# Two heads at once in PEER's routing, one-hots in two operations, and moved gather steps

## The chip, the cores and the metric

One core of a Trainium2 chip runs the kernel. The metric is the device time of one execution in microseconds; the time before is the median of three runs.

## The reference

One decoder layer for 512 tokens of width 1024, in float32: RMSNorm, one combined projection, windowed attention and a gated linear recurrence, their gated merge with a residual, then a PEER layer with its residual and a final RMSNorm. The change touches PEER, which picks 16 of 16384 single-neuron experts per token and head:

```python
def peer_layer(h, w_q, keys, u, v):
    q = (h @ w_q).reshape(B, S, PEER_HEADS, 2, PEER_KEY_DIM)          # 8 heads, two halves
    sc = jnp.einsum('bshpd,phnd->bshpn', q, keys)                     # 128 keys per half
    v1, i1 = lax.top_k(sc[..., 0, :], 16)
    v2, i2 = lax.top_k(sc[..., 1, :], 16)
    cand = v1[..., :, None] + v2[..., None, :]                        # 256 pairs
    best, pos = lax.top_k(cand, 16)
    idx = take_along_axis(i1 * 128 + i2, pos)
    gates = jax.nn.softmax(best)
    act = gelu(einsum('tkd,td->tk', u[idx], h))
    return einsum('tk,tkd->td', gates * act, v[idx])
```

## The kernel before, in words

The layer's first part (projections, attention, recurrence, merge) fills the first 390 us and is not touched, but for the queue of one small load.

PEER is done in two ways. For 160 of the 512 tokens, a block of 128 (`sp0`) and 32 more (`sp1`), the expert rows are gathered: 320 gather steps, each an indirect DMA on POOL of 128 rows of `u` or `v` (L707, 512 KB, four buffers `ga`) and later one step on VectorE that uses them (L715 for `u`, L725 for `v`). `pace` (L727 on) writes gathers up to a given number into the program and, three gathers behind (`GLAG`), their VectorE steps.

For the other 352 tokens (`DT`) the layer is computed densely. For each of 128 chunks of 128 experts, `act_chunk` loads the chunk of `u` (SyncE), splits it into a high part (ScalarE, L142) and a low part (VectorE, L162) and runs 24 matmuls of 352 columns (L646); GELU writes the tile `gel`. The choices of routing become a dense matrix G of gates, 128 by 128 for each token. Then the main loop takes each chunk's `gel` times its slice of G (`w`, L980), splits that too (`whi`, `wlo`), and multiplies it with the chunk of `v` (L994 to L996, 18 matmuls of 512 columns) into six PSUM banks.

The stages in order:

1. Routing (390 to 607 us). For each of 8 heads and 2 halves PE makes queries and scores (L847), VectorE the top 16 of 128 for four token blocks (L854 to L858). After both halves of a head, `route` finds the best 16 pairs: sums of candidates, top 16 of them, softmax on ScalarE, the ranks' arithmetic (L800 to L810), and small float16 one-hots over 16 ranks that pick the key numbers (L816 to L824). It is a generator, resumed by `next(routing)` once per half, so a head's choices run beside the next head's scores. Meanwhile U chunks are written in (`fill`).
2. The G stage (613 to 784). In 22 steps of 16 tokens VectorE writes one-hots of both key numbers over 128 keys (`oh`, L904 to L907, eight tokens at a time; the second is multiplied by the gate's high and low part), PE multiplies them for four tokens at a time into a bank (L912: a weight load and a matmul of 128 columns, 704 of each), ScalarE writes the bank into `G_` (L914), and each step's 1 MB goes to memory (`Gd`, L916). After each bank a quarter of a U chunk's matmuls follows (`piece`). Every third step one gather is added, seven in all.
3. Held U chunks (784 to 819). Of the 53 that there is room for, five (`HELD`) are kept back to cover the last write of Gd and the first read of it (`g_load`, L936). The last two (`LASTU`) are loaded behind that read. Ahead of them `pace(EARLY)` brings the gathers to 16.
4. The main loop, with the remaining U chunks spread over its first 116 chunks and the gathers over all but the last `TAILC`, two.
5. The end: the last three gather steps, then RMSNorm and output of all rows (`final_rows`).

Each engine runs its instructions in the order in which the program has them; the scheduler may interleave what is written, and keeps the matmuls of the G stage in written order. A step that waits on VectorE holds all that is behind it.

Of the kernel before, what the change touches and what calls it, by code (L numbers as in the profile page):

```python
# [6 lines left out]
F32 = mybir.dt.float32  # L7
# [33 lines left out]
QT = 4  # L41
OT = 8
# [7 lines left out]
TAILC = 2  # L50
# [8 lines left out]
def host(inp):  # L59
# [10 lines left out]
    def tm(m):  # L70
# [18 lines left out]
         np.broadcast_to(np.repeat(np.arange(TK, dtype=np.float32), NB), (P, TK * NB)),  # L89
# [27 lines left out]
def layer(nc, tc, a, out, probe=None, upto=99):  # L117
# [37 lines left out]
    def wsplit(raw, shape, parts=1, eng=None):  # L155
        hi = oc.tile(list(shape), F32R, tag="hi", bufs=HB, name=nm("hi"))
        lo = oc.tile(list(shape), F32R, tag="lo", bufs=HB, name=nm("lo"))
        n = shape[1] // parts
        for i in range(parts):
            m = slice(i * n, (i + 1) * n)  # L160
            hi_of(hi[:, m], raw[:, m])
            (eng or V).tensor_tensor(lo[:, m], raw[:, m], hi[:, m].bitcast(F32), op=OP.subtract)  # L162
        return hi, lo
# [28 lines left out]
    with tc.tile_pool(name="front", bufs=1) as fr, tc.tile_pool(name="psf", bufs=1, space=PSUM) as psf:  # L192
# [82 lines left out]
        POOL.dma_start(gm, a["gmix"])  # L275
# [345 lines left out]
    with tc.tile_pool(name="peer", bufs=1) as pp, tc.tile_pool(name="psp", bufs=1, space=PSUM) as psp, ExitStack() as ps:  # L621
# [47 lines left out]

        work = []  # L670

        def piece(limit):
            while len(work) < 2 and nu[0] < limit:
                work.append(act_pieces(next(todo), True))
                next(work[-1])
                nu[0] += 1
            if work and next(work[0], 0) == 0:
                work.pop(0)
# [59 lines left out]
        with tc.tile_pool(name="win", bufs=1) as wp:  # L738
            iota = wp.tile([P, TK, NB], F16, name="iota")
            io32 = wp.tile([P, TK, NB], F32, name="io32")  # L740
            SP.dma_start(io32, a["const"][:, 6 * P:6 * P + TK * NB].rearrange("p (a n) -> p a n", n=NB))
            V.tensor_copy(iota, io32)
            iok32 = wp.tile([P, P, QT], F32, name="iok32")
            SP.dma_start(iok32, a["const"][:, 6 * P + TK * NB:6 * P + TK * NB + P * QT].rearrange("p (i t) -> p i t", t=QT))
# [5 lines left out]
            NK = (P, NB, TK)  # L750

            def route(h, tv, ti):
                hs = slice(h * TK, (h + 1) * TK)
                v1, v2 = tv[:, 0], tv[:, 1]
                cand = w16((P, NB, 64), F32, "cand")
                V.tensor_tensor(cand[:, :, 0:16], v1[:, :, 0:1].to_broadcast([P, NB, 16]), v2, op=OP.add)
                V.tensor_tensor(cand[:, :, 16:40].rearrange("p h (a b) -> p h a b", a=3),
                                v1[:, :, 1:4].unsqueeze(3).to_broadcast([P, NB, 3, 8]),
                                v2[:, :, 0:8].unsqueeze(2).to_broadcast([P, NB, 3, 8]), op=OP.add)
                V.tensor_tensor(cand[:, :, 40:56].rearrange("p h (a b) -> p h a b", a=4),  # L760
                                v1[:, :, 4:8].unsqueeze(3).to_broadcast([P, NB, 4, 4]),
                                v2[:, :, 0:4].unsqueeze(2).to_broadcast([P, NB, 4, 4]), op=OP.add)
                V.tensor_tensor(cand[:, :, 56:64], v1[:, :, 8:16],
                                v2[:, :, 0:1].to_broadcast([P, NB, 8]), op=OP.add)
                best = w16(NK, F32, "best")
                pos = w16(NK, U32, "pos")
                for n in range(NB):
# [18 lines left out]
                k16 = w16((P, 2, TK, NB), F16, "k16")
                for w in range(2):
# [23 lines left out]
                r16 = w16((P, 2, TK, NB), F16, "r16")  # L811
                ACT.activation(r16[:, 0].rearrange("p k n -> p n k"), af, AF.Copy)
                V.tensor_tensor(r16[:, 1].rearrange("p k n -> p n k"), pf, st, op=OP.subtract)
                shape = [P, 2 * TK, TK, NB]
# [6 lines left out]
                                .to_broadcast([P, 2, TK, TK * NB]), op=OP.mult)  # L821
                for m_ in (8, 4, 2):
                    V.tensor_tensor(eq[:, :, 0:m_, :], eq[:, :, 0:m_, :], eq[:, :, m_:2 * m_, :], op=OP.add)
                V.tensor_tensor(i12[:, :, :, hs].rearrange("p w n k -> p w k n"),  # L824
                                eq[:, :, 0, :].rearrange("p (w k) n -> p w k n", w=2),
                                eq[:, :, 1, :].rearrange("p (w k) n -> p w k n", w=2), op=OP.add)
# [3 lines left out]
            for hp in range(2 * PH):  # L830
                h, p_ = divmod(hp, 2)
                if p_ == 0:
                    tv = w16((P, 2, NB, TK), F32, "tv", 3)
                    ti = w16((P, 2, NB, TK), U32, "ti", 3)
# [15 lines left out]
                for n in range(NB):  # L850
                    sc = sb[:, n, :]
                    v_, i_ = tv[:, p_, n, :], ti[:, p_, n, :]
# [6 lines left out]
                if p_ == 1:  # L859
                    routing = route(h, tv, ti)  # L860
# [15 lines left out]
        with tc.tile_pool(name="gb", bufs=1, reuse_waits="tile") as gp:  # L876
# [4 lines left out]
            for n in range(1, NB):  # L881
# [3 lines left out]
                for w in range(2):  # L885
                    PE.transpose(b[:, w, :], i12[:, w, n, :], ident)
# [3 lines left out]
                V.tensor_copy(g16[:, 0, t], gs[:, t])  # L890
                V.tensor_tensor(g16[:, 1, t], gs[:, t], g16[:, 0, t], op=OP.subtract)
            NQ = OT // QT
            shape = [P, NQ, P, QT]
            for s_ in range(NPT):
                G_ = gp.tile([P, NE, TG], F32, tag="G", bufs=2, name=nm("G"))
                for o in range(TG // OT):
                    t = slice(s_ * TG + o * OT, s_ * TG + (o + 1) * OT)

                    def row(x):
                        return x.rearrange("p (q t) -> p q t", t=QT).unsqueeze(2).to_broadcast(shape)  # L900

                    ioq = iok.unsqueeze(1).to_broadcast(shape)
                    oh = gp.tile([P, 3, NQ, P, QT], F16, tag="oh", bufs=2, name=nm("oh"))
                    V.tensor_tensor(oh[:, 0], ioq, row(iT[:, 0, t]), op=OP.is_equal)  # L904
# [142 lines left out]
```

## Time and profile before

| | |
|---|---|
| median of 3 runs | 1666.84 us (1663.52 to 1667.65) |
| the profiled execution, whole | 1675.46 us |
| its span | 1673.7 us |
| PE matmul busy | 1605.2 us, 96% |
| VectorE (DVE) busy | 1321.9 us, 79% |
| ScalarE (ACT) busy | 709.6 us, 42% |
| GpSimd (POOL) busy | 487.3 us, 29% |
| moved by DMA | 400.87 MB, 240 GB/s over the span |

PE is the matmul engine, PEld its weight load. A matmul's row is longer than its share of PE's time, since matmuls overlap; the distance of starts is what one costs. A wait stands in brackets behind the instruction that it delayed, with what ended it. PEclk is the granted share of PE's full clock of 2.4 GHz; 0.50 is 1.2 GHz.

### The profile page before, as it was taken

The page shows a single profiled execution, that of the slowest core. Times are in us where ns is not written, and L with a number is a line of the kernel's source. Part 1 is how long each engine was busy: PE and PEld are TensorE (multiplying, and loading weights), DVE is VectorE, ACT ScalarE, POOL GpSimd, SP SyncE. Part 2 cuts the span into 40 slices and gives each one's busy share as a digit, 9 for nine tenths or more (in the row PEclk, how much of TensorE's full clock was granted, in tenths as well). Part 3 has the DMA queues.
Part 4 walks back from the last instruction along what each step waited for, and adds up shares of the span by engine and source line. Part 5 has one row for each costly group of instructions (what it writes and reads, how often), then busy time and mean ns, then how long its engine had stood idle before and what let it go on. Part 6 is the DMA issues. An engine that isn't in the chain of part 4 may idle for free.

```text
span 1673.7 us, 23435 instructions
## 1 busy us (share of the span) xinstructions
PE 1605.2 (96%) x8511; PEld 1358.7 (81%) x8511; DVE 1321.9 (79%) x2560; ACT 709.6 (42%) x1152; POOL 487.3 (29%) x341
## 2 busy tenths in 40 slices
PE   8999999999999969997899999999999999999996
PEld 6877678888988869997788888887888888888874
DVE  8456663647999988887688888878888888888887
ACT  5433353234554547775333333333333333333333
POOL 4000000000000010002455555445455555554542
PEclk9999999999999979999899999999999999999998
DMA  5311133334333347888999999999999999999984
GB/s 173 101 51 51 51 104 111 103 115 154 108 109 116 103 126 192 219 224 265 336 340 353 349 368 349 337 341 339 344 368 351 359 354 347 360 358 363 343 305 145
DMA packets 197491, 400.87 MB, mean 240 GB/s; under 512 B 103344, under 2 KB 105904, under 8 KB 197376
## 3 DMA queue, kind: packets, MB, share of 16 engines
q1 hardware_dynamic: 58832, 206.02, 35.2%
q0 software_dynamic: 46336, 168.39, 27.0%
q10 hardware_dynamic: 92208, 24.98, 6.1%
q8 instruction: 66, 1.08, 0.3%
q14 instruction: 49, 0.40, 0.1%
HBM read 371.91 MB, written 27.39 MB: 239 GB/s over the span
## 4 chain that ended last, share of the span: by engine, by line
PE 53%; issue 16%; POOL 12%; DVE 12%; DMA 6%; ACT 1%; POOLq 0%; DVEq 0%; SPq 0%; ACTq 0%
PE b L646 13%; POOL ga L707 11%; PE b L263 5%; PE b L262 5%; PE b L995 5%; PE b L996 5%; PE b L265 4%; PE b L994 4%; DMA ga<-v,idx 4%; PE b L912 4%; DVE lo L162 3%; DMA ga<-un,idx 1%; DVE ti L858 1%; DVE mr L856 1%; DVE e L725 1%
## 5 line engine op out<-in xcount | busy, mean ns | idle before, releaser
L707 POOL DMA_INDIRECT ga<-un,idx x160 | 225.2, 1407 | 944.5 <-ACT gs L889 581.3
L646 PE MATMUL b<-hT,hi 128*128 128x352 f32 x2048 | 366.9, 327 | 2.2 <-ACT hi L142 1.7
L646 PEld LDWEIGHTS b<-hT,hi 128*128 128x128 f32 x2048 | 334.4, 190 | 12.7 <-ACT hi L142 2.0
L995 PE MATMUL b<-lo,whi 128*128 128x512 f32 (+1 forms) x768 | 305.0, 397 | 15.0 <-DVE lo L162 14.6
L996 PE MATMUL b<-hi,wlo 128*128 128x512 f32 (+1 forms) x768 | 304.3, 396 | 0.0
L994 PE MATMUL b<-hi,whi 128*128 128x512 f32 (+1 forms) x768 | 302.7, 395 | 0.0
L707 POOL DMA_INDIRECT ga<-v,idx x160 | 240.4, 1502 | 208.3 <-DVE e L725 190.3
L142 ACT ACTIVATE hi<-s 128x1024 fp32r<-128x1024 f32 (+1 forms) x195 | 205.1, 1052 | 203.1 <-PE b L646 88.1
L162 DVE TENSOR_TENSOR lo<-s,hi 128x1024 fp32r<-128x1024 f32 (+1 forms) x195 | 238.5, 1224 | 29.7 <-ACT hi L142 28.0
L142 ACT ACTIVATE whi<-w 128x352 fp32r<-128x352 f32 x128 | 63.7, 498 | 400.0 <-PE b L995 361.2
L725 DVE SCALAR_TENSOR_TENSOR e<-ga,wt,e 128x1024 f32<-128x1024 f32 x158 | 202.2, 1280 | 19.3 <-DMA ga<-v,idx 18.4
L715 DVE SCALAR_TENSOR_TENSOR ga<-ga,h 128x1024 f32<-128x1024 f32 x160 | 194.5, 1220 | 28.6 <-DMA ga<-un,idx 26.9
L646 PE MATMUL b<-hT,lo 128*128 128x352 f32 x1024 | 191.3, 325 | 11.8 <-DVE lo L162 11.8
L995 PEld LDWEIGHTS b<-lo,whi 128*128 128x128 f32 (+1 forms) x768 | 138.8, 181 | 59.2 <-DVE lo L162 22.0
L646 PEld LDWEIGHTS b<-hT,lo 128*128 128x128 f32 x1024 | 168.0, 189 | 12.4 <-DVE lo L162 12.3
L996 PEld LDWEIGHTS b<-hi,wlo 128*128 128x128 f32 (+1 forms) x768 | 138.5, 180 | 39.3
L994 PEld LDWEIGHTS b<-hi,whi 128*128 128x128 f32 (+1 forms) x768 | 138.2, 180 | 35.3 <-ACT hi L142 1.2
L142 ACT ACTIVATE hi<-vr 128x1024 fp32r<-128x1024 f32 x128 | 134.6, 1051 | 75.9 <-PE b L646 46.3
L162 DVE TENSOR_TENSOR lo<-vr,hi 128x1024 fp32r<-128x1024 f32 x128 | 156.1, 1220 | 9.4 <-ACT hi L142 9.4
L263 PE MATMUL b<-hT,hi 128*128 128x512 f32 (+1 forms) x376 | 146.4, 391 | 0.3 <-DVE hT L145 0.3
L262 PE MATMUL b<-hT,hi 128*128 128x512 f32 (+1 forms) x376 | 146.1, 390 | 0.2
L985 DVE TENSOR_TENSOR wlo<-w,whi 128x352 fp32r<-128x352 f32 x128 | 67.0, 523 | 80.9 <-ACT whi L142 77.5
(284 smaller groups left out, 1960.5 us busy)
## 6 DMA issues: line engine op xcount, KB each, us to landing
s<-uc SPq DMA_DIRECT2D x128, 512.0 KB
vr<-vc SPq DMA_DIRECT2D x128, 512.0 KB
Gd<-G ACTq DMA_DIRECT2D x22, 1024.0 KB
gt<-Gd SPq DMA_DIRECT2D x32, 704.0 KB
s<-wfm SPq DMA_DIRECT2D x30, 512.0 KB
s<-wq SPq DMA_DIRECT2D x16, 512.0 KB
s<-wmg SPq DMA_DIRECT2D x8, 512.0 KB
s<-wout SPq DMA_DIRECT2D x8, 512.0 KB
```

Source lines behind the costliest of these rows:

```text
L142: ACT.activation(dst, src, AF.Copy)
L162: (eng or V).tensor_tensor(lo[:, m], raw[:, m], hi[:, m].bitcast(F32), op=OP.subtract)
L262: PE.matmul(b, wh[:, k, :], rh(i), start=start and i == 0, stop=False)
L263: PE.matmul(b, wh[:, k, :], rl(i), start=False, stop=False)
L646: m = PE.matmul(o, w[:, k, :], z[:, k, t], start=i == 0, stop=i == 3 * KD - 1)
L707: tc.keep_in_program_order(POOL.indirect_dma_start(out=t, out_offset=None, in_=a[src], in_offset=bass.IndirectOffsetOnAxis(ap=b.idx[:, j:j ...
L715: V.scalar_tensor_tensor(t, t, 1.0, h20, op0=OP.mult, op1=OP.mult, accum_out=b.act[:, j:j + 1])
L725: V.scalar_tensor_tensor(b.ax, t, b.wt[:, j:j + 1], b.ax, op0=OP.mult, op1=OP.add)
L985: last = V.tensor_tensor(wlo, w, whi.bitcast(F32), op=OP.subtract)
L994: PE.matmul(acc[tb][hf][0:m, :], whi[:, t], vh[:, d], start=i == 0, stop=False)
L995: PE.matmul(acc[tb][hf][0:m, :], whi[:, t], vl[:, d], start=False, stop=False)
L996: PE.matmul(acc[tb][hf][0:m, :], wlo[:, t], vh[:, d], start=False, stop=i == NE - 1)
```

## The change

`route` takes two heads at a time for heads 0 to 5; heads 6 and 7 go singly. Its tiles then hold eight token blocks instead of four, and the top 16 of the candidates, still one block at a time, is cut in two by a second `yield`:

```diff
-            def route(h, tv, ti):
+            def route(h0, tv, ti):
+                NB2 = tv.shape[2]
+                NK = (P, NB2, TK)
+                iota = iotas[NB2]
...
+                    if n == NB - 1 and NB2 > NB:
+                        yield
...
+                two = h < PH - 2
+                if p_ == 0 and not (two and h % 2):
+                    tv = w16((P, 2, NB * (1 + two), TK), F32, "tv", 3)
...
-                if p_ == 1:
-                    routing = route(h, tv, ti)
+                if p_ == 1 and not (two and h % 2 == 0):
+                    for _ in routing:
+                        pass
+                    routing = route(h - two, tv, ti)
```

The one-hots of eight tokens are one tile `[P, 3, P, 8]`, written by two operations. Neighbouring columns of a token's one-hot are now 8 elements of float16 apart, before 4:

```diff
-QT = 4
-OT = 8
+QT = 8
+BT = 4
...
-                    oh = gp.tile([P, 3, NQ, P, QT], F16, tag="oh", bufs=2, name=nm("oh"))
-                    V.tensor_tensor(oh[:, 0], ioq, row(iT[:, 0, t]), op=OP.is_equal)
-                    V.tensor_tensor(oh[:, 2], ioq, row(iT[:, 1, t]), op=OP.is_equal)
-                    V.tensor_tensor(oh[:, 1], oh[:, 2], row(g16[:, 0, t]), op=OP.mult)
-                    last = V.tensor_tensor(oh[:, 2], oh[:, 2], row(g16[:, 1, t]), op=OP.mult)
+                    oh = gp.tile([P, 3, P, QT], F16, tag="oh", bufs=2, name=nm("oh"))
+                    V.tensor_tensor(oh[:, 1:3], ioq, iT[:, :, t].unsqueeze(2).to_broadcast(shape), op=OP.is_equal)
+                    last = V.tensor_tensor(oh[:, 0:2], oh[:, 1:2].to_broadcast(shape),
+                                           g16[:, :, t].unsqueeze(2).to_broadcast(shape), op=OP.mult)
...
-                                lastg = tc.keep_in_program_order(PE.matmul(b[:, i, :], oh[:, 0, q, :, i], oh[:, 1 + w, q, :, i], start=w == 0, stop=w == 1))
+                                lastg = tc.keep_in_program_order(PE.matmul(
+                                    b[:, i, :], oh[:, 2, :, q * BT + i], oh[:, 1 - w, :, q * BT + i],
+                                    start=w == 0, stop=w == 1))
```

Gather steps: one every second step of the G stage (eleven), then one behind each of three held chunks. `piece` may load and split a held chunk ahead of its matmuls:

```diff
-                        piece(KEEP - HELD)
+                        piece(KEEP - HELD, KEEP - HELD + 2)
...
-                pace((s_ + 1) // 3, last.ins)
+                pace((s_ + 1) // 2, last.ins)
...
+        held = cur["lo"]
+        for c_, g_ in work:
+            for _ in g_:
+                pass
+            pace(nga[0] + 1, held.ins)
         with tc.issue_after(lastg.ins):
-            fill(KEEP - nu[0] - LASTU)
+            for _ in range(KEEP - nu[0] - LASTU):
+                fill(1)
+                held = cur["lo"]
+                pace(nga[0] + 1, held.ins)
...
-        pace(EARLY, last.ins)
+        pace(EARLY, held.ins)
```

The end: gathers end three chunks earlier, the gathered block is finished before the last two chunks, and those two are taken bank by bank:

```diff
-TAILC = 2
+TAILC = 5
...
-                    for i, whi, wlo, vh, vl in ready:
-                        for hf in range(2):
-                            d = slice(hf * 512, (hf + 1) * 512)
+                    for hf in range(2):
+                        d = slice(hf * 512, (hf + 1) * 512)
+                        for i, whi, wlo, vh, vl in ready:
...
-        while nsp[0] < NS:
-            sparse(nsp[0])
-            nsp[0] += 1
-        final_rows(ys[0], [sp0.ax[:, 0:512], sp0.ax[:, 512:]], 0, P)
+            if c == NE - 3:
+                while nsp[0] < NS:
+                    sparse(nsp[0])
+                    nsp[0] += 1
+                final_rows(ys[0], [sp0.ax[:, 0:512], sp0.ax[:, 512:]], 0, P)
```

Besides, the constants `io32` and `iok32` are twice as wide, and the load of `gm` at the start is issued by ScalarE instead of POOL.

How the instructions move. VectorE, the last half's maxima of routing (`b_5303` and `b_5173` are its scores) beside head 6's small one-hots (`eq`). Before:

```order
L813 TENSOR_TENSOR r_963_5386<-pf_5238,st_5380 128x4x16
L816 TENSOR_TENSOR eq_5389<-iota,r_963_5386 128x2048
L162 TENSOR_TENSOR lo_5344<-s_955_5341,hi_5343 128x1024
L820 TENSOR_TENSOR eq_5389<-eq_5389,k_935_5235 128x2048
L854 MAX tv_5116<-b_5303 128x8
L823 TENSOR_TENSOR eq_5389<-eq_5389 128x32x32
```

With the change, where the first maximum of `b_5173` stands 24 rows above the first `eq`; this is the block's fourth:

```order
L817 SCALAR_TENSOR_TENSOR st_5250<-af_5244,st_5250 128x64
L870 MAX_INDEX ti_4987<-tv_4986,mr_5278 128x8
L820 TENSOR_TENSOR r_912_5256<-pf_5108,st_5250 128x4x16
L866 MAX tv_4986<-b_5173 128x8
L823 TENSOR_TENSOR eq_5259<-iota_3091,r_912_5256 128x2048
L867 MAX_INDEX ti_4987<-tv_4986,b_5173 128x8
L827 TENSOR_TENSOR eq_5259<-eq_5259,k_884_5105 128x2048
```

Head 6's one-hots and the rank arithmetic moved from before the last half's first maximum to among its maxima.

VectorE, from the last low part of the G stage to the first product with G. `lo` is a U chunk's low part, L715 and L717 are gather steps. Before:

```order
L162 TENSOR_TENSOR lo_7349<-s_1252_7346,hi_7348 128x1024
L715 SCALAR_TENSOR_TENSOR ga_7609,act_3079<-ga_7609,h_62 128x1024
L715 SCALAR_TENSOR_TENSOR ga_7612,act_3079<-ga_7612,h_62 128x1024
L715 SCALAR_TENSOR_TENSOR ga_7615,act_3079<-ga_7615,h_62 128x1024
L715 SCALAR_TENSOR_TENSOR ga_7618,act_3079<-ga_7618,h_62 128x1024
L715 SCALAR_TENSOR_TENSOR ga_7621,act_3079<-ga_7621,h_62 128x1024
L715 SCALAR_TENSOR_TENSOR ga_7624,act_3079<-ga_7624,h_62 128x1024
L162 TENSOR_TENSOR lo_7510<-s_1275_7507,hi_7509 128x1024
L162 TENSOR_TENSOR lo_7542<-s_1279_7539,hi_7541 128x1024
L162 TENSOR_TENSOR lo_7574<-s_1283_7571,hi_7573 128x1024
L980 SCALAR_TENSOR_TENSOR w_7708<-gel_3136,gt_7607 128x352
```

With the change:

```order
L162 TENSOR_TENSOR lo_7149<-s_1205_7146,hi_7148 128x1024
L162 TENSOR_TENSOR lo_7229<-s_1216_7226,hi_7228 128x1024
L717 SCALAR_TENSOR_TENSOR ga_6966,act_3079<-ga_6966,h_62 128x1024
L162 TENSOR_TENSOR lo_7339<-s_1233_7336,hi_7338 128x1024
L717 SCALAR_TENSOR_TENSOR ga_7129,act_3079<-ga_7129,h_62 128x1024
L162 TENSOR_TENSOR lo_7374<-s_1238_7371,hi_7373 128x1024
L717 SCALAR_TENSOR_TENSOR ga_7292,act_3079<-ga_7292,h_62 128x1024
L717 SCALAR_TENSOR_TENSOR ga_7333,act_3079<-ga_7333,h_62 128x1024
L717 SCALAR_TENSOR_TENSOR ga_7368,act_3079<-ga_7368,h_62 128x1024
L1000 SCALAR_TENSOR_TENSOR w_7490<-gel_3138,gt_7410 128x352
```

Three low parts moved up, each ahead of the gather steps that it stood behind, and fewer gather steps are left in the stretch.

VectorE near the end. `lo<-vr` is the low part of a chunk of `v`; L725 and L727 are gather steps, L960 and L980 (with `e` in its name) the additions of `final_rows`. Before:

```order
L985 TENSOR_TENSOR wlo_14974<-w_14970,whi_14972 128x352
L725 SCALAR_TENSOR_TENSOR e_528_3077<-ga_14953,wt_3080,e_528_3077 128x1024
L162 TENSOR_TENSOR lo_14967<-vr_14923,hi_14966 128x1024
L960 TENSOR_TENSOR e_2724_14751<-e_2724_14751,e_528_3077 128x512 x2
L960 TENSOR_TENSOR e_2724_14751<-e_2724_14751,b_7499 128x512
```

With the change, from the last gather step on (`lo_14681` is chunk 124's, and three more follow below):

```order
L727 SCALAR_TENSOR_TENSOR e_528_3077<-ga_14645,wt_3080,e_528_3077 128x1024
L980 TENSOR_TENSOR s_2680_14551<-s_2680_14551,b_14626 32x512
L980 TENSOR_TENSOR s_2680_14551<-s_2680_14551,b_14628 32x512
L162 TENSOR_TENSOR lo_14681<-vr_14596,hi_14680 128x1024
L983 TENSOR_TENSOR rs_14636<-s__2698_14630 32x1
L1005 TENSOR_TENSOR wlo_14688<-w_14684,whi_14686 128x352
L980 TENSOR_TENSOR e_2678_14548<-e_2678_14548,e_528_3077 128x512
```

The last gather step moved from ahead of the last chunk's low part to ahead of that of the fourth from the end, with the gathered rows' final sums behind it.

## Rows read from the trace of the kernel before

**Rows 1.** Windows by stage: start:end length, busy us (instructions) per engine, PEclk, DMA share, GB/s.
```profile
390.00:596.00 206.00, 201.06 (x1118) 182.64 (x1117) 194.26 (x960) 109.06 (x236) 0.00 (x0) 1.00 0.35 115
596.00:613.00 17.00, 2.75 (x13) 2.30 (x14) 13.31 (x35) 7.47 (x27) 3.51 (x3) 0.60 0.30 95
613.00:784.00 171.00, 169.72 (x1229) 157.13 (x1228) 144.89 (x207) 119.15 (x129) 12.25 (x8) 0.99 0.78 213
784.00:819.00 35.00, 22.53 (x124) 21.67 (x122) 19.92 (x30) 10.70 (x15) 14.41 (x10) 0.85 0.96 329
819.00:1640.00 821.00, 810.05 (x4039) 686.65 (x4039) 697.16 (x893) 297.07 (x408) 427.72 (x304) 1.00 0.95 348
1640.00:1674.00 34.00, 19.07 (x71) 13.66 (x69) 22.23 (x34) 10.73 (x29) 9.70 (x1) 0.81 0.34 115
```

**Rows 2.** Timeline of PE after routing: start us, us, engine line op [idle before <-releaser].
```profile
607.29 0.69 PE L886 MATMUL b<-ident,i 128*128 128x128 f32 x2 [11.42 <-DVE i L824]
```

**Rows 3.** Timeline from 784 to 819, and SyncE's waits (total, times, longest).
```profile
799.72 2.71 PE L646 MATMUL b<-hT,lo 128*128 128x352 f32 x8 [10.75 <-DVE lo L162]
...
808.26 0.96 DVE L980 SCALAR_TENSOR_TENSOR w<-gel,gt 128x352 f32<-128x352 f32 x2 [4.51 <-DMA gt<-Gd]
...
818.82 0.40 PE L994 MATMUL b<-hi,whi 128*128 128x512 f32 x1
...
SPq L936 <- DMA Gd<-G: 20.4, 1, 20.4
```

**Rows 4.** Timeline of the last 35 us.
```profile
1639.79 9.91 POOL L707 DMA_INDIRECT ga<-v,idx  x1 [1.89 <-DVE e L725]
...
1653.36 1.28 DVE L725 SCALAR_TENSOR_TENSOR e<-ga,wt,e 128x1024 f32<-128x1024 f32 x1 [4.48 <-DMA ga<-v,idx]
...
1655.84 0.80 PE L995 MATMUL b<-lo,whi 128*128 128x512 f32 x1 [4.04 <-DVE lo L162]
...
1662.71 0.40 PE L996 MATMUL b<-hi,wlo 128*96 128x512 f32 x1
...
1667.34 2.74 DVE L967 SCALAR_TENSOR_TENSOR e<-e,rs,h 128x512 f32<-128x512 f32 x4
```

**Rows 5.** VectorE's groups by shape, 390 to 612 us: count, busy us, mean ns, idle before.
```profile
L816 DVE TENSOR_TENSOR eq<-iota,r 128x2048 f16<-128x2048 f16 x8 | 9.8, 1224 | 0.7
...
L809 DVE TENSOR_TENSOR st<-st,tf 128x64 f32<-128x64 f32 x8 | 1.8, 225 | 0.3
```

**Rows 6.** Timeline of routing's last heads: scores on PE, first maxima and indices on VectorE.
```profile
554.74 1.16 PE L847 MATMUL b<-ky,qp 128*128 128x128 f32 x8 [1.00 <-ACT qp L844]
...
557.93 0.29 DVE L854 MAX8 tv<-b 128x8 f32<-128x128 f32 x1
...
580.30 1.16 PE L847 MATMUL b<-ky,qp 128*128 128x128 f32 x8 [0.84 <-ACT qp L844]
...
583.49 0.29 DVE L854 MAX8 tv<-b 128x8 f32<-128x128 f32 x1
...
607.26 0.49 DVE L865 SCALAR_TENSOR_TENSOR e<-i 128x128 f32<-128x128 f32 x2
```

**Rows 7.** VectorE's first one-hot group by shape, 613 to 784 us; the other three are alike.
```profile
L904 DVE TENSOR_TENSOR oh<-iok,iT 128x1024 f16<-128x1024 f16 x42 | 29.0, 692 | 22.2 <-PE b L912 22.2
```

**Rows 8.** Timeline of weight loads of the one-hots: half clock, then full clock.
```profile
612.70 0.70 PEld L912 LDWEIGHTS <-oh 128*128 128x128 f16 x6 [1.09 <-issue]
...
734.98 0.82 PEld L912 LDWEIGHTS <-oh 128*128 128x128 f16 x8
```

**Rows 9.** ScalarE's groups by shape, 390 to 790 us.
```profile
L914 ACT ACTIVATE G<-b 128x512 f32<-128x512 f32 x88 | 96.0, 1091 | 54.3 <-PE b L912 50.7 <-issue 3.7
...
L844 ACT ACTIVATE qp<-b 128x512 f32<-128x512 f32 x15 | 9.0, 600 | 4.0 <-PE b L265 4.0
```

**Rows 10.** Chain that ended last, pieces: start us, us, what.
```profile
1081.57 3.80 PE b L646 x24
...
1541.08 9.17 DMA ga<-v,idx
```

More of the change, by code (lines that the diff above doesn't have):

```diff
@@ L88, in host @@
          np.full((P, P), 1.0 / P, np.float32),
-         np.broadcast_to(np.repeat(np.arange(TK, dtype=np.float32), NB), (P, TK * NB)),
+         np.broadcast_to(np.repeat(np.arange(TK, dtype=np.float32), 2 * NB), (P, TK * 2 * NB)),
          np.broadcast_to(np.repeat(np.arange(P, dtype=np.float32), QT), (P, P * QT)),
@@ L274, in layer @@
         ktm, logf = [], []
-        POOL.dma_start(gm, a["gmix"])
+        ACT.dma_start(gm, a["gmix"])
         POOL.dma_start(ones, a["const"][:, 5 * P:6 * P])
@@ L670, in layer, with piece @@
         work = []
[L672 to L675, printed above, removed]
+        def piece(limit, ahead):
+            while len(work) < 2 and nu[0] < ahead:
+                c = next(todo)
+                work.append((c, act_pieces(c, True)))
+                next(work[-1][1])
                 nu[0] += 1
-            if work and next(work[0], 0) == 0:
+            if work and work[0][0] < limit and next(work[0][1], 0) == 0:
                 work.pop(0)
@@ L738, in layer @@
         with tc.tile_pool(name="win", bufs=1) as wp:
[L739 to L742, printed above, removed]
+            io32 = wp.tile([P, TK, 2 * NB], F32, name="io32")
+            SP.dma_start(io32, a["const"][:, 6 * P:6 * P + TK * 2 * NB].rearrange("p (a n) -> p a n", n=2 * NB))
+            iotas = {}
+            for n in (NB, 2 * NB):
+                iotas[n] = wp.tile([P, TK, n], F16, name=f"iota{n}")
+                V.tensor_copy(iotas[n], io32[:, :, 0:n])
             iok32 = wp.tile([P, P, QT], F32, name="iok32")
-            SP.dma_start(iok32, a["const"][:, 6 * P + TK * NB:6 * P + TK * NB + P * QT].rearrange("p (i t) -> p i t", t=QT))
+            SP.dma_start(iok32, a["const"][:, 6 * P + TK * 2 * NB:6 * P + TK * 2 * NB + P * QT].rearrange("p (i t) -> p i t", t=QT))
             V.tensor_copy(iok, iok32)
@@ L851, in layer @@
                     sc = sb[:, n, :]
-                    v_, i_ = tv[:, p_, n, :], ti[:, p_, n, :]
+                    n_ = n + NB * (two and h % 2)
+                    v_, i_ = tv[:, p_, n_, :], ti[:, p_, n_, :]
                     m = wp.tile([P, NE], F32, tag="mr", bufs=4, name=nm("mr"))
```

82 lines of the change are left out of this document (39 added, 43 removed).

## The prediction, before the changed kernel ran

> **What bounds the kernel now.** I read the windows by stage first [rows 1]. Look at PE's busy time against each stage's length. From 819 to 1640 us PE is busy 810.05 of 821 us while the DMA engines are busy 0.95 of the time at 348 GB/s. So half of the run is bound by PE, with the transfers close behind it; nothing in the change removes matmuls there. What can be won is PE's idle time elsewhere: 14.2 us from 596 to 613 (2.75 of 17 busy), 12.5 from 784 to 819 (22.53 of 35) and 14.9 from 1640 on (19.07 of 34). The granted clock is 0.60, 0.85 and 0.81 in these three, so after each pause PE also runs for a while at 1.2 GHz. The G stage, 613 to 784, is full: 169.72 of 171 us.
>
> Then I read each hole in the timeline. The first ends when VectorE has written the last expert indices: PE's transposes had waited 11.42 us for it [rows 2]. The second is a wait of 10.75 us of a held U chunk for its low part [rows 3]: VectorE stood in gather steps ahead of that low part in its order. But a second chain runs beside it: SyncE waited 20.4 us for the last write of Gd, and the first product with G, `w`, began only at 808.26 after it [rows 3]. The third is 4.04 us behind the last gather, plus a tail of VectorE work after the last matmul [rows 4].
>
> The profiled execution took 1675.46 us, the median of the three timed runs is 1666.84, so I take 8.6 us off sums made against the profile. About 0.3%, 5 us, is what a measurement of this kernel can tell from no change.
>
> **Part 1: routing for two heads.** For each of three pairs 20 VectorE instructions go away (four for the candidates, the negated best, the reciprocal, eight of the rank arithmetic, six of the small one-hots); their elements stay. An instruction on 64 float32 elements takes 225 ns [rows 5], of which 64 at 0.96 a ns are 67, so 158 ns are saved by each merged one: 60 times 0.158 is 9.5 us of VectorE time. Does it shorten the path? In the last heads both engines turn in the same period: the score matmuls start 25.56 us apart (554.74 and 580.30) and so do the first maxima (557.93 and 583.49), about 2 us after the scores' end [rows 6]. So VectorE can be ahead of PE by 2 us at most before it waits for scores, and PE itself has only 206 minus 201.06, that is 4.9 us, of slack in this stage [rows 1]. Against that, the order shows head 6's small one-hots moved from ahead of the last block's first maximum to behind it. That puts two operations of 1.22 us [rows 5] and six of 0.225, about 3.8 us, into the stretch between the last scores and the indices at 607.26 [rows 6]. Gain and loss cancel; I take 0, with ends of -9.5 (all of the saving lands) and +3.8 (only the move does). If PE does run ahead, it only idles earlier.
>
> **Part 2: one-hots by two operations.** Eight tokens took four operations of 692 ns [rows 7]; two on 2048 elements should take 1.22 each, as the ones of the same size and type do [rows 5]. That is 0.3 us less for 44 groups, 13 us of VectorE time, all beside PE, which is the full engine here; VectorE already waited 22.2 us for PE in this stage [rows 7]. Its cover is PE's 1.9 us per four tokens (171 us over 88 blocks). At the stage's start the first product comes after two long operations instead of three short ones and some casts: -0.6 us.
>
> The price that the trace does not show is on PE. A column of a one-hot now lies 16 bytes from the next, not 8. No PE read with such a step exists in the trace. Below: eight pairs of weight load and matmul take 0.82 us, 102 ns each, although 128 columns at 2.4 GHz are 53 ns; the stream is not what sets the pair, and a slower one may hide: 0. Above: at the half clock, where every column takes twice as long, six loads take 0.70 us, 117 ns each [rows 8]. If both reads halve their rate and overlap as they do there, 704 pairs cost 704 times 0.014, 10 us. ScalarE's rows say that a step can halve a rate: writing G with 64 bytes between elements takes 1091 ns for 512 elements, writing 512 in a row 600 [rows 9]. I take 0, because the nearest row is the pair itself, with half its time unused by the columns.
>
> [...]
>
> **Part 3: gather steps behind held chunks.** Eleven gathers are now issued inside the G stage instead of seven, so five instead of nine are left before the main loop, and on VectorE each held chunk's low part stands before the next gather step. VectorE has room: 144.89 of 171 us busy, minus 13, plus four steps of about 1.2. The wait of 10.75 us goes. What is late next is G: two of the five held chunks, and `w`, are issued behind the read of Gd. Of 34 us between the last block and the first V matmul at 818.82, five chunks of 3.80 us fill 19 [rows 3, 10]. After three chunks PE will be through at about 796 and wait for Gd. That write shares the DMA engines with gathers of 512 KB at 329 GB/s [rows 1]. Four gathers leave this stretch; I count three of them as having run beside the write: 1.57 MB less is 4.8 us. With 1 us from an earlier last block and low part I take -6; ends are 0 (the write takes as long as now) and -12.4 (all idle time but the slow clock's goes). On POOL and SyncE the queues are as before: the same gathers, earlier, and the same loads in the same order.
>
> **Part 4: the main loop.** The gathers end at chunk 122 instead of 125: the same bytes in some 12 us less of 821, so 1.5% more rate at 0.95 busy. PE, now idle 11 us there, may lose some: +2, ends 0 and +8.
>
> **Part 5: the end.** The wait of 4.04 us goes, and with it the slow clock: from 1655.84 to 1662.71 the 23 matmuls started 0.30 us apart, and 512 columns at 2.4 GHz need 0.21 to 0.23, so 1.6 us. Row 0's normalization is done before the last matmul, so one pair of the last scalings (2.74 us for two pairs) leaves the tail: -1.4 [rows 4]. New is a wait for the last gather three chunks earlier: between the step that frees its buffer and its own step lie three gather steps of 1.28 us [rows 4], two low parts of about that length and five short operations, some 8 us, against 9.17 of transfer and its issue [rows 10], so +1.5, since VectorE leads PE by little. Sum -5.5; ends -8.5 and -1.5. The upper end is the last gather meeting VectorE without a pause again: it held POOL for 9.91 us [rows 4].
>
> Two edits are taken at 0: the larger constants load while PE is busy 201 of 206 us, and the 4 KB of mixing gains, now issued by ScalarE, come beside the first weights and tokens; without that cover each costs one transfer's issue.
>
> **Sum.** 0 - 0.6 + 0 - 6 + 2 - 5.5 is -10.1: 1665.4 in a profile, 1657 in the median.
>
> **Rivals.**
> - *The step costs what the half clock costs.* For it: ScalarE's halved rate. Against: the pair's unused half. +10: 1667. Chance 0.17. [...]
> - *Gd is as late as now.* The saved gathers are replaced by others on the same 0.96 busy engines, PE only waits later. For it: the 20.4 us wait. The -6 falls away: 1663. Chance 0.13.
> - *Pairing pays in full.* VectorE is the full engine of routing's last heads (194.26 of 206 busy) and the moved work hides in waits for ScalarE. -9.5: 1648. Chance 0.13.
> - *Slower: the one-hot reads are in series.* Place: each pair in the full G stage. If load and stream both halve and no longer overlap, the pair goes from 102 to some 205 ns: 704 times 0.103 is 72 us, 1729. The point from which it decides is 10.1 + 5 us over 704, that is 21 ns more for a pair, 123 ns. Against it: even the half clock gives 117. Chance 0.12, the values between included.
>
> **How the numbers follow.** The forecast has 0.45, its own range 1652 to 1662. Below it stands the full pairing, above it the late Gd and the step at 10 us; I reach from 1645 to 1670 and leave out the series case and part of the fringes. Faster than 1661.8: nearly all of the forecast and of the pairing case and a third of the late Gd, 0.64. Within 0.3%: the rest of the late Gd and most of the 10 us case, 0.21. Slower: the series case and a little of the step, 0.15.
>
> **What would show it.** Right: PE's pause before the transposes still ends at 605 to 610; 704 pairs of the G stage at 102 ns; no wait of a held chunk for its low part, but one of about 7 us for G near 796; the first V matmul near 811; no 4 us wait before the last matmuls. Wrong: pairs above 115 ns; a first V matmul at 817 or later; transposes at 600; PE idle over 20 us in the main loop.

## The result

The changed kernel takes 1817.2 us (median of 5 runs, 1812.52 to 1818.68) beside 1663.52 us for the kernel before on the same chip: a ratio of 1.0902, 95% interval 1.0882 to 1.0923, some 150 us more. The forecast was 1657, its range 1645 to 1670; the rival on the slower side, with a chance of 0.12, had said 1729.

Windows of the changed kernel, cut at its own stages: start:end length, busy us (instructions) of PE, PEld, VectorE, ScalarE and POOL, granted clock, DMA share, GB/s.

```profile
390.00:596.00 206.00, 200.63 (x1108) 182.53 (x1107) 189.74 (x903) 109.45 (x222) 0.00 (x0) 0.99 0.33 112
607.00:932.00 325.00, 322.71 (x1244) 249.40 (x1243) 142.78 (x133) 124.66 (x136) 19.79 (x13) 0.50 0.44 125
932.00:960.00 28.00, 21.87 (x121) 20.73 (x121) 19.37 (x29) 9.04 (x13) 12.07 (x9) 0.94 0.89 319
960.00:1780.00 820.00, 802.53 (x3993) 681.26 (x3991) 690.58 (x885) 291.25 (x396) 428.60 (x302) 0.99 0.94 346
1780.00:1816.00 36.00, 27.09 (x112) 19.18 (x110) 26.48 (x41) 16.12 (x40) 0.00 (x0) 0.90 0.35 123
```

All stages but one are within 7 us of the length that they had [rows 1]. The G stage, 171 us long before at a clock of 0.99, lasts from 610 to 930 us, and the granted clock is 0.50 all the time: matmuls of 352 columns start 293 ns apart in it, 1.20 columns a ns, and 161 ns apart in the kernel before. PE is counted as busy in 322.71 of 325 us, so no wait shows where the time went; the distances of starts do. The timeline of PE at the start of the stage and in its middle:

```profile
605.65 0.69 PE L900 MATMUL b<-ident,i 128*128 128x128 f32 x2 [8.77 <-DVE i L834]
...
610.12 2.02 PE L921 MATMUL b<-oh 128*128 128x128 f16 x8 [2.29 <-DVE oh L915]
...
700.99 2.07 PE L921 MATMUL b<-oh 128*128 128x128 f16 x8
702.70 2.12 PE L646 MATMUL b<-hT,hi 128*128 128x352 f32 x6
704.63 2.08 PE L921 MATMUL b<-oh 128*128 128x128 f16 x8
```

The same three rows of the kernel before:

```profile
736.91 1.11 PE L912 MATMUL b<-oh 128*128 128x128 f16 x8
737.77 1.22 PE L646 MATMUL b<-hT,hi 128*128 128x352 f32 x6
738.83 1.11 PE L912 MATMUL b<-oh 128*128 128x128 f16 x8
```

A bank takes 3.64 us (700.99 to 704.63), not 1.92: its eight pairs of weight load and matmul 1.71, that is 214 ns each and not 107 (0.86 us for eight), and its quarter of a U chunk 1.93 instead of 1.06. Over 88 banks the 1.72 us are 151 us, the whole of the loss. Two other steps of the prediction are in the trace as they were foretold: the pause ahead of the transposes ends at 605.65, against 607.29 [rows 2], and the two operations of VectorE take 1225 ns for 2048 elements, where one of the four took 692 for 1024 [rows 7]:

```profile
L914 DVE TENSOR_TENSOR oh<-iok,iT 128x2048 f16<-128x2048 f16 x44 | 53.9, 1225 | 170.2 <-PE b L921 169.4 <-ACT iT L902 0.8
```

So two things are to be explained: why a pair takes twice its time, and why the clock stays at its lower level through 320 us of work.

### The profile page after: what moved, and what is told of

Read it like the earlier page. It is cut to its first block, busy times and chain, and to the rows that moved or that the text cites. A ratio compares the mean times of both kernels' runs of the same rounds, so it can differ in the third digit from the quotient of the medians.

```text
span 1815.4 us, 23255 instructions
## 1 busy us (share of the span) xinstructions
PE 1757.0 (97%) x8511; PEld 1449.2 (80%) x8511; DVE 1307.9 (72%) x2413; ACT 711.6 (39%) x1131; POOL 479.0 (26%) x340
## 4 chain that ended last, share of the span: by engine, by line
PE 64%; issue 15%; DVE 8%; DMA 7%; POOL 5%; ACT 1%; DVEq 0%; POOLq 0%; ACTq 0%
PE b L646 18%; PE b L1015 6%; PE b L1016 6%; PE b L1014 6%; PE b L263 5%; PE b L262 5%; PE b L265 5%; POOL ga L709 5%; PE b L921 5%; DMA ga<-v,idx 4%; DVE lo L162 2%; DMA ga<-un,idx 1%; DVE e L727 1%; DMA vr<-vc 1%; PE b L858 1%
## 5 line engine op out<-in xcount | busy, mean ns | idle before, releaser
L646 PE MATMUL b<-hT,hi 128*128 128x352 f32 x2048 | 420.5, 358 | 3.8 <-ACT hi L142 3.3
L646 PEld LDWEIGHTS b<-hT,hi 128*128 128x128 f32 x2048 | 377.5, 212 | 20.1 <-ACT hi L142 3.9
L709 POOL DMA_INDIRECT ga<-v,idx x160 | 231.9, 1449 | 214.3 <-DVE e L727 198.8
L646 PE MATMUL b<-hT,lo 128*128 128x352 f32 x1024 | 219.1, 358 | 7.2 <-DVE lo L162 7.2
L727 DVE SCALAR_TENSOR_TENSOR e<-ga,wt,e 128x1024 f32<-128x1024 f32 x158 | 202.1, 1279 | 17.4 <-DMA ga<-v,idx 17.2
L717 DVE SCALAR_TENSOR_TENSOR ga<-ga,h 128x1024 f32<-128x1024 f32 x160 | 194.3, 1219 | 18.9 <-DMA ga<-un,idx 17.2
L646 PEld LDWEIGHTS b<-hT,lo 128*128 128x128 f32 x1024 | 191.1, 213 | 10.0 <-DVE lo L162 8.1
L921 PE MATMUL b<-oh 128*128 128x128 f16 x704 | 182.4, 416 | 2.3 <-DVE oh L915 2.3
L914 DVE TENSOR_TENSOR oh<-iok,iT 128x2048 f16<-128x2048 f16 x44 | 53.9, 1225 | 170.2 <-PE b L921 169.4
L925 ACT ACTIVATE G<-b 128x512 f32<-128x512 f32 x88 | 95.1, 1080 | 183.9 <-PE b L921 183.9
```

The costliest lines, as they stand in the source:

```text
L646: m = PE.matmul(o, w[:, k, :], z[:, k, t], start=i == 0, stop=i == 3 * KD - 1)
L709: tc.keep_in_program_order(POOL.indirect_dma_start(out=t, out_offset=None, in_=a[src], in_offset=bass.IndirectOffsetOnAxis(ap=b.idx[:, j:j ...
L717: V.scalar_tensor_tensor(t, t, 1.0, h20, op0=OP.mult, op1=OP.mult, accum_out=b.act[:, j:j + 1])
L727: V.scalar_tensor_tensor(b.ax, t, b.wt[:, j:j + 1], b.ax, op0=OP.mult, op1=OP.add)
L921: lastg = tc.keep_in_program_order(PE.matmul(b[:, i, :], oh[:, 2, :, q * BT + i], oh[:, 1 - w, :, q * BT + i], start=w == 0, stop=w == 1))
L925: ACT.activation(G_[:, :, m:m + BT].rearrange("p c t -> p t c"), b, AF.Copy)
```

## Experiments

Twelve kernels ran, numbered in the order in which they went to the chip, and told here by question. Ratios are to the kernel before on the same chip.

### 1 and 2: is it the layout of the one-hots?

Experiment 1 is the change with the old step between columns:

```diff
-QT = 8
+QT = 4
-                    oh = gp.tile([P, 3, P, QT], F16, tag="oh", bufs=2, name=nm("oh"))
+                    oh = gp.tile([P, 3, P, QT], F16, tag="oh", bufs=4, name=nm("oh"))
```

> The whole change, but the one-hots are laid out for four tokens, so that their columns lie 8 bytes apart as before; the two operations then write four tokens each. Theory A (the 16-byte step slows PE's reads, and the slow reads keep the clock at half): a bank of the G stage takes 1.92 us again, the granted clock is 1.00 in it, and about 150 of the 154 us go: 1655 to 1668 us. Theory B (the clock stays at half for another reason in the change, such as how the stage is entered): a bank stays at 3.64 us, about 1815.

Experiment 2 is the kernel before with nothing but the part of the diff from `QT` to the matmuls on `oh`.

> The kernel before with the one-hots of the change alone (two operations for eight tokens, columns 16 bytes apart). Theory A: banks of 3.64 us at a granted clock of 0.50, 1810 to 1825 us. Theory B: banks of about 1.92 us and no change, 1655 to 1670.

The first took 1669.38 us, a ratio of 1.0006 (0.9989 to 1.0024); the second 1807.31, 1.0835 (1.0799 to 1.0871). Theory A holds from both sides: with the old step the loss is gone, and everything else in the change together moves nothing that can be measured; with the new step alone the kernel before loses 139 us. The 11 us that are left between 1.0835 and 1.0902 were not tried by themselves; 1807.31 is also a little under the 1810 to 1825 that A gave. PE in experiment 1, a bank of the G stage and then the held chunks:

```profile
775.11 1.11 PE L921 MATMUL b<-oh 128*128 128x128 f16 x8
...
777.03 1.11 PE L921 MATMUL b<-oh 128*128 128x128 f16 x8
...
800.07 4.39 PE L646 MATMUL b<-hT,hi 128*128 128x352 f32 x16 [7.42 <-ACT hi L142]
...
809.37 0.39 PE L1014 MATMUL b<-hi,whi 128*128 128x512 f32 x1
```

A bank is back at 1.92 us. (The last two rows are used further down.)

### 3 and 7: why the clock stays low

Experiment 3 keeps PE busy in the pause at the end of routing, with matmuls that nobody reads:

```diff
             fill(2)
+            bw = bank()
+            for i in range(60):
+                tc.keep_in_program_order(PE.matmul(bw[:, :DT], zh[:, 0, 0:P], zh[:, 0, T0:S], start=i == 0, stop=i == 59))
```

> The changed kernel with 60 matmuls of 352 columns, whose result nobody uses, ahead of the transposes, so that PE is busy in the pause and enters the G stage at the full clock. Theory A1 (slow reads whatever the clock, and the clock falls because of them): the clock falls back to 0.50 within the first banks, 1805 to 1825 us. Theory A2 (slow reads whatever the clock, but a full clock once reached is held): banks of 1.71 + 0.97 = 2.7 us, 88 times 0.96 us less than now, about 1733. Theory B: pairs of about 107 ns and pieces of 0.97 us once the clock is full, about 1665.

It took 1815.28 us, 1.0883 (1.0849 to 1.0917): no gain, as A1 had it. But its windows show that the clock, full from 604 on, fell at 611.3, just behind a gap that was left, 2.92 us between the transposes and the first one-hots at 610.09:

```profile
604.00:608.00 4.00, 3.17 (x23) 2.90 (x21) 2.51 (x6) 1.88 (x8) 1.18 (x2) 1.00 0.02 2
608.00:612.00 4.00, 1.92 (x9) 1.47 (x10) 3.97 (x10) 0.00 (x0) 3.39 (x3) 0.91 0.81 246
612.00:616.00 4.00, 4.00 (x17) 3.16 (x17) 0.85 (x2) 1.29 (x2) 0.18 (x1) 0.50 0.76 279
```

So the run did not tell whether the slow pairs bring the clock down or only fail to bring it up. Experiment 7 closes that gap too, with 24 more such matmuls behind the transposes.

> The changed kernel with idle matmuls ahead of the transposes and 24 more behind them, so that PE does not pause at all before the first one-hot. Theory H (both levels of the clock hold themselves: the mix of slow pairs and dense pieces keeps a full clock but does not lift a half one): banks of 1.71 + 1.17 = 2.9 us at a granted clock of 1.00, 88 times 0.76 us less than now: 1740 to 1755 us. Theory A1 (the mix itself lowers the clock): back at 0.50 within some banks, 1805 to 1820.

It took 1751.4 us, 1.0519 (1.0496 to 1.0543). Its window of the whole G stage, and three rows of PE within:

```profile
610.00:865.00 255.00, 255.00 (x1250) 190.68 (x1250) 140.01 (x127) 120.81 (x131) 16.56 (x11) 1.00 0.55 156
```

```profile
700.31 2.07 PE L927 MATMUL b<-oh 128*128 128x128 f16 x8
702.01 1.32 PE L646 MATMUL b<-hT,lo 128*128 128x352 f32 x6
703.18 2.07 PE L927 MATMUL b<-oh 128*128 128x128 f16 x8
```

The same banks now run at a granted clock of 1.00 for 255 us. Theory H holds: entered at 1.00 this mix keeps 1.00, entered at 0.50, as in the changed kernel, it stays at 0.50 for 320 us. And eight pairs take 1.70 us at 1.00 and 1.71 at 0.50, so their 214 ns don't come from the clock. That splits the loss: 2.87 us for a bank against 1.92 is 84 us for the reads, 3.64 against 2.87 is 68 us for the clock. (Of the 0.95 us for the reads 0.84 are in the pairs, the rest in the dense matmuls behind them.) The ratios say the same: 0.0519 of 1664 is 86, and 0.0383 more is 64.

### 4 and 8: which read, and at what step

Two kernels, one execution of each, add bursts behind the last output of the kernel before; the operands are views of a tile of zeros. In `pairs(128, ks, km)` the steps count float16 elements of two bytes, `ks` for the weights and `km` for the other operand of the matmul, the moving one:

```diff
+        def col(k):
+            return zf[:, 0:P * k].rearrange("p (c k) -> p c k", k=k)[:, :, 0]
...
+        for ks, km in ((4, 4), (8, 8), (8, 4), (4, 8), (16, 16), (1, 1)):
+            dense(40, 512)
+            pairs(128, ks, km)
```

> The kernel before with, behind its last output, bursts of 128 pairs of weight load and matmul of 128 float16 columns (zeros), each burst behind 40 dense matmuls of 512 columns; the step between columns of weights/moving operand is 8/8, 16/16, 16/8, 8/16, 32/32 and 2/2 bytes; then 16 times eight pairs and six matmuls of 352 columns, at 8/8 and at 16/16. Its extra work takes some 200 us. Theory A: at the full clock a pair takes about 107 ns at 8/8 and about 214 at 16/16, some 160 where only one operand has the wide step, and the clock falls to 0.50 in the mixed burst at 16/16 but not at 8/8. Theory B: all pairs take about 107 ns while the clock is full.

> The kernel before with bursts of 128 pairs behind its last output, each behind 40 dense matmuls: steps of weights/moving operand of 8/4, 8/2, 4/4, 8/12, 2/16 and 8/8 bytes; then VectorE writes of 1024 one-hot elements with 8, 4, 2 and 1 tokens innermost. Theory S: pairs near 57 + 8 ns for each byte beyond 2 of the moving step (8/4 75, 8/2 60, 4/4 75, 8/12 165, 2/16 220 ns), and the weights' step hardly counts. Theory L: 8/4 as 8/8, and 8/12 already as 8/16. VectorE: 692 ns with 8, 4 and 2 tokens innermost, about 1.1 us with one.

Timeline of PE in experiment 4, four bursts of 128 pairs (L1050) and the dense matmuls between:

```profile
1662.42 15.38 PE L1050 MATMUL b<-ga 128*128 128x128 f16 x128
1677.55 9.36 PE L1043 MATMUL b<-hi 128*128 128x512 f32 x40
1686.75 30.18 PE L1050 MATMUL b<-ga 128*128 128x128 f16 x128
1716.57 10.94 PE L1043 MATMUL b<-hi 128*128 128x512 f32 x40
1727.35 15.80 PE L1050 MATMUL b<-ga 128*128 128x128 f16 x128
1742.91 9.37 PE L1043 MATMUL b<-hi 128*128 128x512 f32 x40
1752.12 29.65 PE L1050 MATMUL b<-ga 128*128 128x128 f16 x128
1781.41 10.98 PE L1043 MATMUL b<-hi 128*128 128x512 f32 x40
```

The distance from a burst's start to the next row, over 128, is the time of a pair: 118 ns with both steps at 8 bytes, 233 with both at 16, 122 with only the weights at 16, 229 with only the moving operand at 16. Theory A's 160 for one wide operand was wrong: the moving operand carries the whole cost, the weights next to nothing. With those not shown, worked out in the same way:

| step of weights / moving operand, bytes | ns for a pair |
|---|---|
| 2 / 2 | 56 |
| 8 / 2 | 56 |
| 4 / 4 | 57 |
| 8 / 4 | 60 |
| 8 / 8 | 118 |
| 8 / 12 | 173 |
| 2 / 16 | 225 |
| 8 / 16 | 229 |
| 32 / 32 | 239 |

Up to 4 bytes the step costs next to nothing; at 8 the pair has doubled, at 16 doubled again, and 32 adds little. (That 8 bytes give 118 ns here and 107 in the kernel is a matter of counting: in the trace of before, from the second on, the starts within a group of eight are 115 to 122 ns apart too, but the dense matmul starts 47 ns behind the eighth.) Neither theory S nor L of experiment 8 fits below 8 bytes: the 75 ns of S for 8/4 were too many, and L had 8/4 equal to 8/8. Two burst rows of experiment 8, at 8/4 and 8/12:

```profile
1663.68 7.82 PE L1050 MATMUL b<-ga 128*128 128x128 f16 x128
1671.31 9.35 PE L1043 MATMUL b<-hi 128*128 128x512 f32 x40
...
1713.32 22.50 PE L1050 MATMUL b<-ga 128*128 128x128 f16 x128
1735.51 10.71 PE L1043 MATMUL b<-hi 128*128 128x512 f32 x40
```

The clock, in windows of experiment 4 at the start of the 16/16 burst, in the rest of it, and in the last mix of eight pairs at 16/16 and six dense matmuls:

```profile
1687.00:1690.00 3.00, 3.00 (x14) 1.90 (x13) 0.00 (x0) 0.00 (x0) 0.00 (x0) 1.00 0.00 0
1690.00:1716.00 26.00, 26.00 (x112) 16.17 (x111) 0.00 (x0) 0.00 (x0) 0.00 (x0) 0.55 0.00 1
...
1900.00:1934.00 34.00, 34.00 (x167) 25.42 (x167) 0.00 (x0) 0.00 (x0) 0.00 (x0) 1.00 0.00 0
```

The window counts matmuls that reach into it, so its 14 are not a time; single starts of this burst are 235 ns apart on the average before the clock falls, at 1692.7, and 233 after it. So the level does not matter to such a pair here either. In the burst of slow pairs alone the clock falls, to 0.55 on the average from 1690 on; mixed with dense work, and entered at 1.00, it stays at 1.00 to the end at 1934, against A's expectation and as in experiment 7.

VectorE in experiment 8 writes 1024 one-hot elements with 8, 4 and 2 tokens innermost (L1063, three operations in a row) and with one (L1066):

```profile
1667.54 2.14 DVE L1063 TENSOR_TENSOR ga<-ga,ga 128x1024 f16<-128x1024 f16 x3
1669.72 1.22 DVE L1066 TENSOR_TENSOR ga<-ga,ga 128x1024 f16<-128x1024 f16 x1
```

So two tokens innermost, a step of 4 bytes, cost VectorE nothing (0.71 us each), one token costs 1.22.

### 6: the step the other way

The kernel before reads at 8 bytes, 118 ns for a pair in the bursts against 57 at 4, and so pays already. Experiment 6 is that kernel with two tokens innermost, the banks still of four:

```diff
-QT = 4
 OT = 8
+QT = 2
+BT = 4
...
+                            j, k = divmod(q * BT + i, QT)
+                                lastg = tc.keep_in_program_order(PE.matmul(b[:, i, :], oh[:, 0, j, :, k], oh[:, 1 + w, j, :, k], start=w == 0, stop=w == 1))
```

> The kernel before with one-hots laid out for two tokens, so that neighbouring columns lie 4 bytes apart. The bursts showed 57 ns for a pair at 2 bytes, 120 at 8 and 231 at 16 for the moving operand. Theory S (the time of a read grows with the bytes between columns): a pair takes 60 to 85 ns, a bank 1.45 to 1.65 us, and the G stage shortens by 20 to 35 us unless VectorE, 145 of 171 us busy there, or the transfers take over: 1632 to 1652 us. [...]

1645.28 us, 0.9891 (0.9876 to 0.9907), within what S gave for the whole; its pairs are a little under the 60 to 85 ns of S. A bank:

```profile
635.57 0.64 PE L914 MATMUL b<-oh 128*128 128x128 f16 x8
636.01 1.20 PE L647 MATMUL b<-hT,lo 128*128 128x352 f32 x6
637.05 0.64 PE L914 MATMUL b<-oh 128*128 128x128 f16 x8
```

1.48 us, its pairs 55 ns each. Of the 39 us that 88 banks would save, some 18 arrive: VectorE is now busy 131.32 of the 137 us from 613 to 750, and from 600 to 800 us PE waits for it, 7.8 us in all for one-hots and 13.7 for low parts of U chunks. ScalarE waits 34.6 us for writes of Gd; in the kernel before it has no such wait.

### 5, 9 and 12: the other parts

Experiment 5 is experiment 1 with the end of the kernel before (`TAILC = 2`, the gathered block and the last chunks as they were), 9 is 5 with the gathers' pace of the change alone, 12 is 5 with the pairing of heads undone.

```diff
 experiment 9, on 5
-TAILC = 2
+TAILC = 5
 experiment 12, on 5
-                two = h < PH - 2
+                two = 0
```

> The change with columns 8 bytes apart (as in the first experiment) and with the end of the kernel as before: gathers up to the last two chunks, the gathered block finished at the end, the last chunks in the old order. Theory M (the earlier end of the gathers costs the main loop what the new end saves): the stretch from the first V matmul to the last matmul is some 6 us shorter than the 842.6 of that experiment, the end behind the last matmul is 10.5 us again, and the whole is 0.2 to 0.4% faster than before. Theory N (the main loop's length varies from run to run and the new end does save its 5 us): 0.2 to 0.4% slower than before.

> The kernel of the fifth experiment (columns 8 bytes apart, the end as before, 0.9945 of before) with one number changed: the gathers are spread up to the fifth chunk from the end again, as in the change; the gathered block is still finished at the end. Theory P (the denser gathers cost the main loop): the V matmuls' waits for a low part go from 7 us back to some 15, and the time to 0.998 to 1.002 of before. Theory Q (it is the work placed ahead of the last two chunks, or their order, that costs): 0.992 to 0.996 as in the fifth experiment.

> The kernel of the fifth experiment (0.9945 of before) with all eight heads routed singly, that is with the pairing of heads undone. The prediction took the pairing at nothing: then 0.993 to 0.996 again, and PE's pause ahead of the transposes ends within 2 us of 604.98. If the pairing pays its 9.5 us of VectorE time, this run loses them: 0.999 to 1.001 of before, the transposes at about 614; if it pays a part, in between.

Measured: 5 took 1655.88 us, 0.9945 (0.9931 to 0.9958); 9 took 1668.91, 1.0012 (0.9994 to 1.003); 12 took 1653.72, 0.9928 (0.9914 to 0.9941). So pairing gains nothing: without it the time is the same or a little less (0.9928, just under the 0.993 to 0.996 that were expected), and the transposes start at 604.62 against 604.98. And the denser gathers cost 0.67% of 1665, 11 us, theory P (and M, though the 0.55% of experiment 5 are more than its 0.2 to 0.4). The waits of PE for low parts of V chunks in the main loop (total us, times, longest), in experiments 5 and 9:

```profile
PE b L1015 <- DVE lo L162: 7.2, 9, 2.1
```

```profile
PE b L1015 <- DVE lo L162: 19.3, 15, 3.1
```

Experiment 1, with the pace and the new end, has 15.8 in 18 waits, and it and 9 don't differ in time (1.0006 and 1.0012): what the new end does apart from the pace is worth nothing that these runs separate, although the stretch behind the last matmul falls from 10.4 us in 5 to 8.3 in 1. One caution: these waits vary between executions of one kernel. The profiled execution of before has 14.6 us of them at the old pace, and it was a long one; the verdict rests on the ratios. Why a denser pace delays low parts was not tried by itself; that VectorE stands in gather steps ahead of them is argued from the order only.

### 10 and 11: a kernel that beats both

Experiment 10 puts together what paid: the held chunks of the change, the old end, and two tokens innermost with both comparisons in one operation.

```diff
 on experiment 5
-iT = gp.tile([P, 2, DT], F16, name="iT")
+iT = gp.tile([P, DT // OT, 2, OT], F16, name="iT")
...
+oh = gp.tile([P, 3, NQ, P, QT], F16, tag="oh", bufs=2, name=nm("oh"))
+V.tensor_tensor(oh[:, 1:3].rearrange("p w q c t -> p (w q) c t"), ioq,
+                iT[:, n].rearrange("p w (q t) -> p (w q) t", t=QT).unsqueeze(2).to_broadcast(shape), op=OP.is_equal)
+for w in range(2):
+    last = V.tensor_tensor(oh[:, w], oh[:, 1], g16[:, n, w].rearrange("p (q t) -> p q t", t=QT).unsqueeze(2).to_broadcast([P, NQ, P, QT]), op=OP.mult)
```

> What the runs speak for, together: columns 4 bytes apart (two tokens innermost), pairing of heads and held chunks from the change, the end as before; the comparison of both key numbers in one VectorE operation, the two products in one each. If the gains add: 0.9891 less 0.0055, that is 0.983 to 0.985 of before, 1636 to 1641 us, with banks of 1.48 us and PE waiting for VectorE in the G stage. If VectorE is the bound there, one of 1.22 us in place of two of 0.69 gives 0.16 us for eight tokens, 7 us for 44: down to 0.979.

> The same with both products in one VectorE operation as well, on an access of four free dimensions. If that operation takes 1.22 us like the other of 2048 elements, another 0.16 us for eight tokens, up to 7 us less than the run beside it; if the fourth dimension slows it, slower than that run.

1634.93 us, 0.9829 (0.9795 to 0.9863), and 1638.66, 0.9833 (0.9808 to 0.9858). The gains add, and 31 us are gone against before, some 180 against the change. Shorter work on VectorE gives no more. The windows of the G stage in experiments 10 and 11:

```profile
613.00:755.00 142.00, 130.25 (x1181) 115.83 (x1178) 136.99 (x162) 102.69 (x123) 11.80 (x8) 0.99 0.94 252
613.00:755.00 142.00, 128.50 (x1177) 115.93 (x1177) 132.32 (x120) 104.12 (x124) 12.69 (x8) 0.98 0.97 256
```

VectorE is busy 136.99 of 142 us in 10 and 132.32 in 11, and the 4.7 us less bring nothing. The DMA engines are full in both, 0.94 and 0.97 of the time, 0.78 in the kernel before [rows 1]. PE now waits for high parts of U chunks, and ScalarE, which writes them, waits for writes of Gd, whose tile it fills anew. From experiment 10, the totals and a place where one wait follows on the other:

```profile
PE b L647 <- ACT hi L143: 17.7, 10, 4.4
ACT G L930 <- DMA Gd<-G: 36.1, 12, 4.1
...
695.82 1.07 ACT L930 ACTIVATE G<-b 128x512 f32<-128x512 f32 x1 [3.56 <-DMA Gd<-G]
696.68 1.06 ACT L143 ACTIVATE hi<-s 128x1024 fp32r<-128x1024 f32 x1
697.79 1.22 PE L647 MATMUL b<-hT,hi 128*128 128x352 f32 x6 [0.88 <-ACT hi L143]
```

In 11 these waits are 23.1 us of PE and 27.1 of ScalarE. That the writes now limit the stage is read from these rows; no run changed them.

## Why the prediction was wrong

**Part 2, the step that failed.** "I take 0, because the nearest row is the pair itself, with half its time unused by the columns." The pair's 107 ns were read as a fixed time under which a slower stream could hide. The bursts show that they hang on the step of the moving operand: at 4 bytes the pair takes 57. No half of its time was free, and doubling the step doubled the pair to 214 ns. The upper end of 10 us had the same fault: it took the pair at the half clock as a price for half the rate, but eight pairs at 16 bytes take 1.70 us at a granted clock of 1.00 and 1.71 at 0.50. The rows of before showed it already: 0.82 us for eight loads and 0.70 for six [rows 8] were divided by eight and six, to 102 and 117 ns, but from the second on the single matmuls of such a group start 115 to 122 ns apart at either level, and only the first distance and the one behind the last differ. So the 14 ns of that end were no price of the clock. The term of the sum was 0 and measures 84 us.

**What no case had: the clock.** The other 68 us come from the lower level being kept. The prediction named the slow stretches around pauses as a price of some us each and took for granted that PE climbs back, as it had in the same stage before, 0.99 over its whole length [rows 1]. With the slow pairs it stayed at 0.50 until the dense held chunks behind 930 (0.94 from 932 to 960).

**The slower rival** had the right place and nearly the right size for a pair (205 ns), hence 72 us against 84. Its mechanism was not the right one: load and stream need not be in series, since the moving operand alone does it. Its own evidence against, "even the half clock gives 117", was the sign that the pair hung on the read.

**Part 1, right.** Taken at 0 with ends of -9.5 and +3.8; experiment 12 against 5 is -0.17%, with intervals that overlap, and the pause ended in the foretold 605 to 610, or just ahead of it. VectorE did get shorter, 191.75 us busy from 390 to 600 in 5 and 197.70 in 12 for 60 instructions more, so 99 ns for each and not 158, and PE gained nothing by it, as the prediction argued.

**Part 3, right.** In experiment 1 no held chunk waits for its low part, a wait of 7.42 us for the loads behind G stands in its place (7 foretold), and the first V matmul starts at 809.37 (811 foretold), against 818.82 before [rows 3]. Without parts 4 and 5 and with the old step, experiment 5 gains 0.55%, 9 us, where -6.6 was summed for them and the earlier first one-hot.

**Part 4, mis-sized.** +2 with ends of 0 and +8 was taken for the denser gathers; 9 against 5 is 11 us. "1.5% more rate at 0.95 busy" sounded small; why it cost more than its +8 stays open.

**Part 5, not shown as a gain.** -5.5 was summed; apart from the pace, the new end moves nothing measurable. The 4.04 us wait near the end, on which most of it rested, did not come back: in the five runs with the old end (5, 6, 10, 11, 12) PE waits 0.4 us at most for a low part behind 1580 us. It had been read from the longest execution of before, 1675.46 us.

So without part 2 the sum would have been -9.5, and experiment 1 measured +1 (-2 to +4): part 3 came, part 4 took it back, and part 5 did not come.

## What to carry to other kernels

Before the layout of a matmul's moving operand is changed, put its column step in bytes beside the time of a matmul: if that is above what as many columns take at a step of 2 bytes (56 ns here for a pair with 128), suspect the read, and measure a burst of such matmuls at half and at double the step. PE "busy" in all of a window says nothing of speed (322.71 of 325 us here at a clock of 0.50); the granted clock and the distance of starts do. And ask of each stage at which level of the clock it is entered, and whether its own mix brings it up.

## Not expected of the hardware

- The moving operand's step costs next to nothing up to 4 bytes (56 to 60 ns for a pair of 128 float16 columns), costs 118 ns at 8, 173 at 12, 229 at 16 and 239 at 32; the weights' step costs 4 ns at 16 bytes.
- One mix of work held either level of PE's clock: 0.50 for 320 us in the changed kernel, 1.00 for 255 us in experiment 7, and a pause of 2.92 us ahead of it is all that 3, which had 0.50, has beyond 7.
- VectorE writes one-hots as quickly with two elements in a row as with eight (0.71 us for 1024), and with one it takes 1.22.
